# A decoder layer with three attention branches: causal masks moved from TensorE to the softmax bias and into a scan, and the first feed-forward products reordered

## The chip, the cores and the metric

The kernel runs on one core of one Trainium2 chip. Its engines are TensorE (PE in the profile, its weight loads PEld), VectorE (DVE), ScalarE (ACT), GpSimd (POOL) and SyncE (SP, which issues most DMAs). Each engine works through its own queue in order; semaphores order the engines against each other. The metric is the device time of one execution in microseconds (us), the median of several runs.

## The reference

One layer, 1024 tokens of width 1024, all in float32:

```python
proj = x @ w_in            # queries, keys, values of three branches, an index head group, gates
o_a  = sparse attention    # top-256 keys by the index score, softmax with ALiBi, 8 heads
o_b  = forgetting attention # softmax(q k / 8 + c_q - c_k), causal: key <= query, 8 heads
# stick-breaking, 8 heads, strictly causal (key < query):
z = q k / 8
log_one_minus = where(key < query, log_sigmoid(-z), 0)
later = reverse cumulative sum of log_one_minus, without the element itself
a = where(key < query, exp(log_sigmoid(z) + later), 0)
o_c = a v
merged = sum over branches of (o_i w_branch_i) * sigmoid(gates_i)
x  = LN1(alpha * x + merged w_out)
h  = relu(x w_ff1) ** 2
out = LN2(alpha * x + h w_ff2)
```

## The kernel before, in words

Dense products are done in three parts: each float32 operand is split into a high part (a conversion on ACT or POOL) and a low part (a subtraction on DVE or POOL), and hi*hi, hi*lo and lo*hi are added up in PSUM. `split` and `Weights.convert` do this; `wraw` is the weight as loaded, `whi` and `wlo` its parts.

The kernel has these stages: transposing x; the index products and scores; the three attention branches in the order Fox (forgetting), Stick (stick-breaking), Dsa (sparse), with the projections and gates of the input matrix run between their steps as filler; the branch products; the output product with the first layer norm; the first feed-forward product; the second one.

An attention unit (`Unit`) is one head and two query tiles of 128 rows (`u` from 0 to 3, tiles 2u and 2u+1). Its steps: `qk` makes the scores of one row tile against all keys up to its diagonal, in one or two PSUM banks named `l` (two exist); `rows` turns them into weights; `tr` transposes pairs of blocks on PE into banks named `t` and splits them into `ph` and `pl`; `pv` multiplies with the values into a bank `o`.

In `qk` the causal mask is a third product into the same bank: the weights `negeye` (-1e30 on the diagonal, bf16) times a triangle of ones, `tri_excl` (keys after the query) for Fox and for the first two tiles of Dsa, `tri_incl` (the query's own key too) for Stick.

`softmax_rows` (Fox and Dsa) adds the bias and takes the running extreme on DVE, `tensor_tensor_reduce`, which the profile calls CUSTOM_DVE_ANT_0 (out `p`, and `nm` for the extreme). Then the exponential runs on ACT, the reciprocal of the sum on DVE, and the scaling on POOL (`p<-p,sm`). Fox's bias `ct` is one row of 1024 running sums, broadcast to 128 partitions by a DMA, one tile a head; Dsa's `bt` is made on POOL. In Stick, ACT makes two sigmoids `u` and `be`, DVE runs a scan from the last key to the first (`u<-u,zero`), and POOL multiplies.

What stands where in a queue is decided in two steps. A planner (`Plan`) keeps a clock for each engine with written-out costs; `drive` picks the attention step that is ready on that clock, or a step of filler. A search for the top-256 threshold of each query row (`select`: 33 rounds of six counts `jk`, then six passes that write the bias into `score`) is put in the background of DVE wherever the planner sees a gap; what is left when Dsa needs a row is emitted at once. The framework then orders each engine's instructions by its own list scheduling.

The first feed-forward product is done with seven block products per group of 256 columns instead of eight, from sums and differences of blocks of x (`x1` to `x7`, each as `h` and `l`) and of the weights (`hl`); `PSTEPS` is the order of the products. The blocks of x come from transposes of the normalised rows (`transpose_row`, evicted to `mr`) and their sums (`sums`). For the last row tile this happens inside the loop over `PSTEPS`, at step 2, followed by all splits of blocks 5, 7, 4 and 3.

## Time and profile before

| | |
|---|---|
| runs | 2045.75 us median of 3 (2042.17 to 2050.64) |
| profiled execution | 2043.96 us, of which the span from first to last instruction is 2042.2 us |
| granted TensorE clock, mean of the span | 0.995 of full speed |
| PE busy | 2007.3 us (98%) |
| DVE busy | 1391.3 us (68%) |
| ACT busy | 981.8 us (48%) |
| POOL busy | 479.7 us (23%) |

Busy time is the union of an engine's instructions. Products on PE overlap, so the length of one is more than the time between two starts. A time in square brackets behind a row is the engine's idle time ahead of it, with the instruction that ended it. The granted clock is given as a share of full speed; the two levels are 1.2 and 2.4 GHz.

### The profile page before, as it was taken

The numbers are of one execution on the slowest core, as the hardware profiler recorded it, in microseconds if no ns is written. First come the engines' busy times: TensorE is split into PE (matmuls) and PEld (weight loads), VectorE is DVE, ScalarE is ACT, GpSimd is POOL, SyncE is SP. The second block draws the span as 40 slices with busy tenths as digits, with TensorE's granted clock in tenths as the row PEclk, the third lists the DMA queues.
The fourth block names the chain that finished last, engine by engine and source line by source line (L and its number), as shares of the span: only waits on it lengthen the run. The fifth ranks groups of instructions, "written<-read, shape, count | busy, mean of one in ns | idle before, by whom it ended". The sixth has DMA issues, their size and how long they took to land. (4 is left out here: it accounts for less than half of the span.)

```text
span 2042.2 us, 30020 instructions
## 1 busy us (share of the span) xinstructions
PE 2007.3 (98%) x10534; PEld 1693.5 (83%) x10534; DVE 1391.3 (68%) x2501; ACT 981.8 (48%) x1913; POOL 479.7 (23%) x460
## 2 busy tenths in 40 slices
PE   8999999999999999999999999999999999999998
PEld 7788889888888888878988888887877787888886
DVE  3785487777788888764343356767788866875557
ACT  5573454445464464344454443445444445644443
POOL 3312322333353453554354204000000000000003
PEclk9999999999999999999999999999999999999999
DMA  5434534344234334243352586621699845986653
GB/s 158 101 78 99 122 88 122 91 116 108 69 94 120 75 83 116 68 112 91 83 118 74 161 283 204 223 73 46 238 331 347 324 147 196 332 270 191 195 176 124
DMA packets 210327, 308.71 MB, mean 151 GB/s; under 512 B 22248, under 2 KB 116456, under 8 KB 208128
## 3 DMA queue, kind: packets, MB, share of 16 engines
q1 hardware_dynamic: 196032, 281.09, 46.5%
q10 hardware_dynamic: 14144, 25.70, 3.5%
q8 instruction: 83, 1.36, 0.3%
q14 instruction: 68, 0.56, 0.1%
HBM read 182.89 MB, written 79.79 MB: 129 GB/s over the span
## 5 line engine op out<-in xcount | busy, mean ns | idle before, releaser
L138 PE MATMUL d<-xh,whi 128*128 128x512 f32 (+1 forms) x912 | 316.8, 399 | 3.5 <-ACT g__9749 L138 1.2
L138 PE MATMUL d<-xh,wlo 128*128 128x512 f32 (+1 forms) x912 | 312.0, 393 | 0.0
L138 PE MATMUL d<-u 128*128 128x512 f32 x1320 | 303.0, 391 | 2.5 <-ACT u L138 1.8
L138 PE MATMUL d<-xl,whi 128*128 128x512 f32 (+1 forms) x912 | 304.8, 385 | 0.0
L138 PEld LDWEIGHTS d<-u 128*128 128x128 f32 x1320 | 248.4, 188 | 56.9 <-ACT u L138 3.2
L138 POOL TENSOR_TENSOR wlo<-wraw,whi 128x512 fp32r<-128x512 f32 x138 | 196.8, 1429 | 386.9 <-ACT whi L138 345.2
L138 DVE TENSOR_TENSOR u<-sr,u 128x512 fp32r<-128x512 f32 x220 | 144.7, 702 | 91.1 <-ACT u L138 90.9
L138 DVE TENSOR_TENSOR pl<-t,ph 128x512 fp32r<-128x512 f32 (+1 forms) x240 | 146.6, 630 | 85.8 <-ACT ph L138 85.5
L138 ACT ACTIVATE u<-sr 128x512 fp32r<-128x512 f32 x220 | 130.1, 627 | 142.0 <-PE d L138 105.4
L138 PEld LDWEIGHTS d<-xl,whi 128*128 128x128 f32 x912 | 172.4, 189 | 30.9
L138 POOL TENSOR_TENSOR z<-z,res 128x512 f32<-128x512 f32 x14 | 19.7, 1429 | 748.0 <-ACT z L138 733.1
L138 PEld LDWEIGHTS d<-xh,whi 128*128 128x128 f32 x912 | 167.6, 190 | 29.6 <-DVE st L138 2.2
L138 DVE TENSOR_SCALAR_CACHE_REDUCE jk<-sc,fb 128x384 uint8<-128x384 f32 (+2 forms) x198 | 186.2, 940 | 3.4
L138 PEld LDWEIGHTS d<-xh,wlo 128*128 128x128 f32 x912 | 164.2, 190 | 25.6
L138 ACT ACTIVATE ph<-t 128x512 fp32r<-128x512 f32 (+1 forms) x240 | 127.7, 558 | 94.3 <-PE t L138 88.7
L138 ACT ACTIVATE p<-p,nm 128x896 f32<-128x896 f32 (+7 forms) x128 | 99.3, 776 | 148.7 <-DVE nm L138 132.5
L138 ACT ACTIVATE whi<-wraw 128x512 fp32r<-128x512 f32 x136 | 86.3, 634 | 160.3 <-PE d L138 114.0
L138 POOL TENSOR_SCALAR p<-p,sm 128x896 f32<-128x896 f32 (+7 forms) x128 | 98.6, 772 | 147.1 <-DVE sm L138 143.4
L138 DVE TENSOR_TENSOR_SCAN u<-u,zero 128x128 f32<-128x128 f32 (+3 forms) x64 | 110.5, 1737 | 24.0 <-ACT u L138 23.2
L138 PE MATMUL o<-ph,v 128*128 128x256 f32 x480 | 121.5, 278 | 0.0
L138 PE MATMUL o<-pl,v 128*128 128x256 f32 x480 | 118.2, 284 | 1.9 <-DVE pl L138 1.5
L138 ACT ACTIVATE mr<-mr 128x512 f32<-128x512 f32 x110 | 69.3, 630 | 85.7 <-DVE mr L138 83.6
(274 smaller groups left out, 4394.5 us busy)
## 6 DMA issues: line engine op xcount, KB each, us to landing
wraw<-in_w_in_dram SPq DMA_DIRECT2D x136, 256.0 KB, 3.0
sr<-h_scratch SPq DMA_DIRECT2D x112, 256.0 KB, 3.3
w1raw<-in_w_ff_dram SPq DMA_DIRECT2D x16, 1024.0 KB, 6.8
h_scratch<-mr SPq DMA_DIRECT2D x64, 256.0 KB, 3.6
w2raw<-in_w_ff_dram SPq DMA_DIRECT2D x16, 1024.0 KB, 7.7
t_scratch<-w2raw SPq DMA_DIRECT2D x16, 1024.0 KB, 8.1
sr<-t_scratch SPq DMA_DIRECT2D x64, 256.0 KB, 4.0
oraw<-o_scratch SPq DMA_DIRECT2D x24, 512.0 KB, 4.9
```

The lines of the kernel that those rows point to most:

```text
L138: r = f(*args, **kw)
```

## The change

- `qk` has no mask product any more; `negeye` and both triangles are gone.
- Fox: the mask is written into the bias. A head's units run from u = 3 down to 0 and a unit's tiles from the higher to the lower (`down`). At a head's first row POOL writes -1e30 over the part of the last 128-column block of `ct` that lies after the query (`diagonal`); after the reduction of row i, and ahead of its exponential, it does the same to the block before, for row i-1. The blocks behind need no repair, since lower rows don't read them. `prepare` loads the next head's `ct` one head ahead.
- Dsa: for the first two tiles POOL writes the mask into `bt`; the others had no mask product.
- Stick: the scan runs over the keys 1 to w-1, with maximum in place of addition and a byte tile `newest` in place of zeros. `newest` holds a one at each query's newest key, so that the running product begins there, and zeros elsewhere. The last column of `be` is set to zero by a memset on DVE.
- First feed-forward: the last row tile is transposed at step 1, PE's products 1 to 5 are pinned in order behind its transposes, and the splits of blocks 5, 7, 4 and 3 are spread over steps 3, 4, 6 and 7.
- Small things: `zero` and `bf` share a tile, as do `fb`, `mb`, `cnt` and `need` (`sel`).

The diff, cut to its core:

```diff
-    negeye = cp.tile([P, P], BF16, name="negeye")
-    V.tensor_scalar(negeye, ident, -BIG, None, op0=ALU.mult)
-    tri_incl = cp.tile([P, P], BF16, name="tri_incl")
-    tri_excl = cp.tile([P, P], BF16, name="tri_excl")
-    for t_, cmp in ((tri_excl, ALU.is_gt), (tri_incl, ALU.is_ge)):
-        V.memset(t_, 1.0)
-        G.affine_select(t_, t_, pattern=[[1, P]], compare_op=cmp, fill=0.0, base=0,
-                        channel_multiplier=-1)
+    newest = cp.tile([P, S], U8, name="newest")
+    def diagonal(t_, cmp, fill):
+        G.affine_select(t_, t_, pattern=[[-1, P]], compare_op=cmp, fill=fill, base=0, channel_multiplier=1)
...
+    one = plan.tile(ap, [P, S], F32, tag="T", bufs=2, name="one")
+    V.memset(one, 0.0)
+    G.affine_select(one[:, S - P - 1:S - 1], one[:, S - P - 1:S - 1], pattern=[[-1, P]],
+                    compare_op=ALU.not_equal, fill=1.0, base=0, channel_multiplier=1)
+    V.tensor_copy(newest, one)
...
@@ -519,11 +523,8 @@
         cut = min(w, 384 if w == 640 else 512)
         for c, tag in zip((slice(0, cut), slice(cut, w))[:1 + (cut < w)], tags):
             dst = bank(tag, 2)[:, :c.stop - c.start]
-            last = mask is not None and c.stop == w
             for n, (q, k) in enumerate((first, second)):
-                T.matmul(dst, q[:, qs], k[:, c], start=n == 0, stop=n == 1 and not last)
-            if last:
-                T.matmul(dst[:, i * P - c.start:], negeye, mask, start=False, stop=True)
+                T.matmul(dst, q[:, qs], k[:, c], start=n == 0, stop=n == 1)
             out.append((c, dst))
         return out
...
-    def softmax_rows(lg, i, bias):
+    def softmax_rows(lg, i, bias, then=None):
         w = (i + 1) * P
         p = row_tile(i, "p")
         sm = plan.tile(ap, [P, 1], F32, tag="sm", bufs=4, name="sm")
@@ -566,24 +567,36 @@
             nm = plan.tile(ap, [P, 1], F32, tag="nm", bufs=4, name="nm")
             V.tensor_tensor_reduce(p[:, c], l_, bias[:, c], -SCALE, m, ALU.add, ALU.min, nm)
             m = nm
+        if then:
+            then()
         A.activation(p[:, :w], p[:, :w], AF.Exp, bias=nm, scale=-1.0, accum_out=sm)
         V.reciprocal(sm, sm)
         G.tensor_scalar(p[:, :w], p[:, :w], sm, 0.0, op0=ALU.mult, op1=ALU.add)
         return p
     class Fox:
-        branch, mask = 1, lambda self, i: tri_excl
+        branch, down = 1, True
+        def __init__(self):
+            self.ct = []
         def prepare(self, h):
-            ct = plan.tile(ap, [P, S], F32, tag="T", bufs=2, name="ct")
-            Q.dma_start(ct, c_dram[h:h + 1, :].broadcast_to([P, S]))
-            return ct
+            for n in range(len(self.ct), min(NH, h + 2)):
+                self.ct.append(plan.tile(ap, [P, S], F32, tag="T", bufs=2, name="ct"))
+                Q.dma_start(self.ct[n], c_dram[n:n + 1, :].broadcast_to([P, S]))
+            diagonal(self.ct[h][:, S - P:], ALU.is_ge, -BIG)
+            return self.ct[h]
         def rows(self, lg, i, h, ct):
-            return softmax_rows(lg, i, ct[:, :(i + 1) * P])
+            def mask():
+                if i > 0:
+                    diagonal(ct[:, (i - 1) * P:i * P], ALU.is_ge, -BIG)
+            return softmax_rows(lg, i, ct[:, :(i + 1) * P], mask)
     class Stick:
-        branch, mask = 2, lambda self, i: tri_incl
+        branch, down = 2, False
         prepare = pre = None
         def rows(self, lg, i, h, _):
@@ -593,13 +606,16 @@
             for c, l_ in lg:
                 A.activation(u[:, c], l_, AF.Sigmoid, scale=-SCALE)
                 A.activation(be[:, c], l_, AF.Sigmoid, scale=SCALE)
-            V.tensor_tensor_scan(u[:, :w][:, ::-1], u[:, :w][:, ::-1], zeros(P, w), 1.0,
-                                 ALU.mult, ALU.add)
+            V.tensor_tensor_scan(u[:, 1:w][:, ::-1], u[:, 1:w][:, ::-1], newest[:, S - w:S - 1][:, ::-1], 0.0,
+                                 ALU.mult, ALU.max)
+            V.memset(be[:, w - 1:w], 0.0)
             G.tensor_tensor(be[:, :w - 1], be[:, :w - 1], u[:, 1:w], ALU.mult)
             return be
     class Dsa:
-        branch, mask = 0, lambda self, i: None if i in TI else tri_excl
+        branch, down = 0, False
         prepare = pre = None
         def rows(self, lg, i, h, _):
...
                        allow_small_or_imprecise_dtypes=True)
             G.tensor_scalar(bt[:, :w], d, -slope / SCALE, 0.0, op0=ALU.mult, op1=ALU.add)
+            if i not in TI:
+                diagonal(bt[:, i * P:w], ALU.is_ge, -BIG)
             return softmax_rows(lg, i, bt[:, :w])
     class Unit:
...
+        def tile(self):
+            n = len(self.p)
+            return 2 * self.u + (1 - n if self.kind.down else n)
         def qk_ready(self):
             pr, r = self.pair, self.h % 2
-            return max(qk_slot(2 * self.u + len(self.p)), plan.slot(ap, f"P{2 * self.u + len(self.p)}", 1),
+            return max(qk_slot(self.tile()), plan.slot(ap, f"P{self.tile()}", 1),
                        plan.ready(pr["q"][r], pr["qs", r], pr["k"][r]))
         def qk(self):
             k = self.kind
             n, pr, r = len(self.p), self.pair, self.h % 2
-            if n == 0 and self.u == 0 and k.prepare:
+            if n == 0 and self.u == 3 * k.down and k.prepare:
                 k.pre = k.prepare(self.h)
-            i = 2 * self.u + n
-            lg = qk((pr["q"][r], pr["k"][r]), (pr["qs", r], pr["k"][r]), i, k.mask(i))
-            self.p.append(k.rows(lg, i, self.h, k.pre))
+            i = self.tile()
+            lg = qk((pr["q"][r], pr["k"][r]), (pr["qs", r], pr["k"][r]), i)
+            self.p.insert(0 if k.down else n, k.rows(lg, i, self.h, k.pre))
         def tr_ready(self):
             return max(plan.slot(ps, "t", 2), plan.slot(ap, "ph", 2), plan.ready(*self.p))
...
@@ -812,12 +833,13 @@
-    def order(first):
-        return [(r, u) for v in range(2) for r in range(2) for u in (2 * v, 2 * v + 1)] if first else \
-            [(r, u) for r in range(2) for u in range(4)]
+    def order(k, p):
+        if k is kinds[2] and p == 0:
+            return [(r, u) for v in range(2) for r in range(2) for u in (2 * v, 2 * v + 1)]
+        return [(r, u) for r in range(2) for u in (range(3, -1, -1) if k.down else range(4))]
     units = [Unit(k, 4 * n + p, pairs[4 * n + p], 2 * p + r, u) for n, k in enumerate(kinds)
-             for p in range(NPAIR) for r, u in order(n == 2 and p == 0)]
+             for p in range(NPAIR) for r, u in order(k, p)]
     qks = [(m, n) for m in range(len(units)) for n in range(2)]
     trs = [(m, jp) for m, un in enumerate(units) for jp in range(un.u + 1)]
     st = {"qk": 0, "tr": 0, "pv": 0, "swap": 0}
...
@@ -1297,17 +1322,24 @@
     AHEAD = 3
     W2_AT = [16 + 6 * n for n in range(NPR)]
+    LATER = {3: (b11, 5), 4: (b12, 7), 6: (b21, 4), 7: (b22, 3)}
     prepare1(2)
     for m in range(len(PSTEPS)):
-        if m == 2:
-            transpose_row(NT - 1, (A, V))
+        if m == 1:
+            behind = transpose_row(NT - 1, (A, V))
             sums(3)
-            for src, j in ((b11, 5), (b12, 7), (b21, 4), (b22, 3)):
-                for c in range(4):
-                    ts_ = slice(c * P, (c + 1) * P)
-                    split(*(v[:, :, ts_] for v in x1v[j]), src[:, :, ts_])
+        if m in LATER:
+            src, j = LATER[m]
+            for c in range(4):
+                ts_ = slice(c * P, (c + 1) * P)
+                split(*(v[:, :, ts_] for v in x1v[j]), src[:, :, ts_])
         prepare1(m + AHEAD)
-        product1(m)
+        if 1 <= m <= 5:
+            with tc.issue_after(behind.ins):
+                behind = product1(m)
+        else:
+            product1(m)
         evacuate1(*PSTEPS[m])
         if m == W2_AT[0] - 2:
             rctx.close()
```

Where the instructions stand, before and after. First POOL in Fox, around the change from one head's rows to the next's (`p<-p,sm` is the scaling of one row tile, its width the row's; `wlo<-wraw,whi` the low part of a filler weight). Before:

```order
L138 TENSOR_SCALAR p<-p,sm 128x1024
L138 TENSOR_TENSOR wlo<-wraw,whi 128x512
L138 TENSOR_SCALAR p<-p,sm 128x128
L138 TENSOR_SCALAR p<-p,sm 128x256
L138 TENSOR_SCALAR p<-p,sm 128x384
L138 TENSOR_SCALAR p<-p,sm 128x512
L138 TENSOR_TENSOR wlo<-wraw,whi 128x512
```

After, from row tile 3 of the first head to row tile 6 of the second:

```order
L138 TENSOR_SCALAR p<-p,sm 128x512
L138 TENSOR_SCALAR p<-p,sm 128x384
L138 AFFINE_SELECT ct<-ct 128x128
L138 TENSOR_TENSOR wlo<-wraw,whi 128x512
L138 TENSOR_SCALAR p<-p,sm 128x256
L138 TENSOR_SCALAR p<-p,sm 128x128
L138 AFFINE_SELECT ct<-ct 128x128 x2
L138 TENSOR_SCALAR p<-p,sm 128x1024
L138 TENSOR_TENSOR wlo<-wraw,whi 128x512
L138 AFFINE_SELECT ct<-ct 128x128
L138 TENSOR_SCALAR p<-p,sm 128x896
```

The rows run downwards now, and between the scalings stand the selects that write the mask for the next row; the first of the two selects that stand together at a head's begin belongs to another head's bias.

Second PE at the first feed-forward products, at the first product with block 6 of x (`x1`, `x2`, `x6` name the block; each product is a run of twelve). Before:

```order
L138 MATMUL d<-x1l,hl 128x512
L138 MATMUL d<-x1h,hl 128x512
L138 MATMUL d<-x6h,hl 128x512
L138 MATMUL d<-x6l,hl 128x512
L138 MATMUL d<-x6h,hl 128x512 x2
L138 MATMUL d<-x6l,hl 128x512
```

After:

```order
L138 MATMUL d<-x2h,hl 128x512 x2
L138 MATMUL d<-x2l,hl 128x512
L138 MATMUL d<-x2h,hl 128x512
L138 MATMUL d<-x6h,hl 128x512
L138 MATMUL d<-x6l,hl 128x512
L138 MATMUL d<-x6h,hl 128x512 x2
L138 MATMUL d<-x6l,hl 128x512
```

Before, block 6 follows the second product of block 1; now the second product of block 2 stands between them.

Third DVE in the same place (`x5l`, `x7l`, `x4l`, `x3l` are the low parts of blocks of x, `hl` those of weights, `s` and `w1raw` sums of weights, `mr<-d,early` an eviction). Before:

```order
L138 TENSOR_TENSOR x6l<-t_15155,x6h 128x4x128
L138 TENSOR_TENSOR x5l<-mr,x5h 128x4x128 x2
L138 TENSOR_TENSOR x7l<-mr,x7h 128x4x128 x4
L138 TENSOR_TENSOR x4l<-mr,x4h 128x4x128 x4
L138 TENSOR_TENSOR x3l<-mr,x3h 128x4x128 x4
L138 TENSOR_TENSOR hl<-w1raw,hl 128x512
L138 TENSOR_TENSOR hl<-s_15098,hl 128x512
L138 TENSOR_TENSOR mr<-d,early 128x512
L138 TENSOR_TENSOR s_15339<-w1raw 128x512
L138 TENSOR_TENSOR w1raw<-w1raw 128x4x128 x3
```

After:

```order
L138 TENSOR_TENSOR x6l<-t_15310,x6h 128x4x128
L138 TENSOR_TENSOR x5l<-mr,x5h 128x4x128 x4
L138 TENSOR_TENSOR hl<-s_15253,hl 128x512
L138 TENSOR_TENSOR x7l<-mr,x7h 128x4x128 x4
L138 TENSOR_TENSOR s_15478<-w1raw 128x512
L138 TENSOR_TENSOR mr<-d,early 128x512
L138 TENSOR_TENSOR w1raw<-w1raw 128x4x128
L138 TENSOR_TENSOR x4l<-mr,x4h 128x4x128
L138 TENSOR_TENSOR w1raw<-w1raw 128x4x128
L138 TENSOR_TENSOR x4l<-mr,x4h 128x4x128 x2
L138 TENSOR_TENSOR hl<-w1raw,hl 128x512 x2
L138 TENSOR_TENSOR x4l<-mr,x4h 128x4x128
```

Before, all sixteen low parts of blocks 5, 7, 4 and 3 stand ahead of the next weights; now those of block 4 stand among the weight sums, and those of block 3 further behind.

## Rows read from the trace of the kernel before

**Rows 1.** The page: busy time of PE, and its share in 40 slices (tenths).

```profile
PE 2007.3 (98%) x10534; PEld 1693.5 (83%) x10534; DVE 1391.3 (68%) x2501; ACT 981.8 (48%) x1913; POOL 479.7 (23%) x460
...
PE   8999999999999999999999999999999999999998
```

**Rows 2.** Busy time by stretch: start:end, then its length and the engines' shares.

```profile
core 0: us, PE busy (x) PEld busy (x) DVE busy (x) ACT busy (x) POOL busy (x), PEclk, DMA share, GB/s
200.00:525.00 325.00, 324.51 (x1984) 282.21 (x1983) 223.01 (x605) 147.66 (x309) 96.86 (x102) 1.00 0.42 104
525.00:790.00 265.00, 262.50 (x1610) 223.75 (x1609) 222.91 (x313) 156.28 (x348) 127.86 (x98) 1.00 0.36 88
790.00:900.00 110.00, 104.28 (x595) 90.58 (x594) 89.15 (x170) 36.39 (x77) 46.33 (x49) 0.97 0.43 103
900.00:1110.00 210.00, 210.00 (x1260) 185.61 (x1259) 87.70 (x249) 99.98 (x207) 97.00 (x124) 1.00 0.38 93
...
1398.00:1424.00 26.00, 22.44 (x91) 16.71 (x90) 24.87 (x45) 17.51 (x35) 0.00 (x0) 0.93 0.11 42
```

**Rows 3.** Instructions that read `negeye`: shortest, median and longest in ns.

```profile
L138 PE MATMUL l<-tri_excl,negeye x80: 229/230/233, 221.8 to 1109.8; 128*128 128x128 bf16 x80
L138 PE MATMUL l<-tri_incl,negeye x64: 229/230/234, 531.9 to 779.1; 128*128 128x128 bf16 x64
```

**Rows 4.** PE in order of time at a mask: start, length in us.

```profile
222.14 0.23 PE L138 MATMUL l<-tri_excl,negeye 128*128 128x128 bf16 x1
222.18 0.48 PE L138 MATMUL d<-xh,whi 128*128 128x512 f32 x1
222.50 0.39 PE L138 MATMUL d<-xl,whi 128*128 128x512 f32 x1
```

**Rows 5.** PE in order of time behind index scores, which have no mask.

```profile
47.12 0.40 PE L138 MATMUL d<-xh,whi 128*128 128x512 f32 x1
47.36 0.39 PE L138 MATMUL d<-xl,whi 128*128 128x512 f32 x1
47.59 0.39 PE L138 MATMUL d<-xh,wlo 128*128 128x512 f32 x1
```

**Rows 6.** Instructions on the tile `score` (`sc`): counts on DVE, selects on POOL.

```profile
L138 DVE TENSOR_SCALAR_CACHE_REDUCE jk<-sc,fb x198: 580/938/1281, 176.5 to 830.6; 128x384 uint8<-128x384 f32 x33, 128x512 uint8<-128x512 f32 x33, 128x640 uint8<-128x640 f32 x33, 128x768 uint8<-128x768 f32 x33
...
L138 POOL TENSOR_SCALAR_AFFINE_SELECT sc<-sc x6: 292/679/1007, 170.7 to 176.4; 128x128 f32<-128x128 f32 x6
```

**Rows 7.** POOL's waits in Fox, 200 to 525: total us, times, longest.

```profile
POOL wlo L138 <- ACT whi L138: 85.7, 22, 25.1
```

**Rows 8.** The tile `ct`, Fox's bias: its eight loads.

```profile
DMA to landing us min/median/max: 3.4/4.5/5.7
```

**Rows 9.** Instructions on the tile `zero`: scans of Stick, a one-column memset.

```profile
L138 DVE TENSOR_TENSOR_SCAN u<-u,zero x64: 414/1749/3848, 533.9 to 780.6; 128x128 f32<-128x128 f32 x8, 128x256 f32<-128x256 f32 x8, 128x384 f32<-128x384 f32 x8, 128x512 f32<-128x512 f32 x8
...
L138 DVE MEMSET zero<- x1: 59/59/59, 0.9 to 0.9; 128x1 f32 x1
```

**Rows 10.** PE's waits from 790 to 900, the begin of Dsa.

```profile
PE l L138 <- DVE nm L138: 4.4, 3, 2.5
```

**Rows 11.** PE and DVE in order of time at the first feed-forward products.

```profile
1398.86 0.39 PE L138 MATMUL d<-x1h,hl 128*128 128x512 f32 x1
...
1402.07 0.85 PE L138 MATMUL d<-ident,row 128*128 128x128 f32 x5 [0.33 <-DVE row L138]
...
1410.20 0.50 PE L138 MATMUL d<-x6h,hl 128*128 128x512 f32 x1 [1.43 <-ACT x6h L138]
1411.35 0.74 PE L138 MATMUL d<-x6l,hl 128*128 128x512 f32 x1 [0.64 <-DVE x6l L138]
...
1414.82 2.49 DVE L138 TENSOR_TENSOR x4l<-mr,x4h 128x512 fp32r<-128x512 f32 x4
...
1417.23 2.49 DVE L138 TENSOR_TENSOR x3l<-mr,x3h 128x512 fp32r<-128x512 f32 x4
...
1425.61 0.40 PE L138 MATMUL d<-x6h,hl 128*128 128x512 f32 x1
```

More of the change, by code (lines that the diff above doesn't have):

```diff
@@ L189, in trunk @@
     make_identity(nc, ident)
-    zero = cp.tile([P, 1], F32, name="zero")
+    both = cp.tile([P, 2], F32, name="both")
+    zero, bf = both[:, 0:1], both[:8, 1:2]
     V.memset(zero, 0.0)
     A.activation(zero, zero, AF.Copy)
-    negeye = cp.tile([P, P], BF16, name="negeye")
-    V.tensor_scalar(negeye, ident, -BIG, None, op0=ALU.mult)
-    tri_incl = cp.tile([P, P], BF16, name="tri_incl")
-    tri_excl = cp.tile([P, P], BF16, name="tri_excl")
-    for t_, cmp in ((tri_excl, ALU.is_gt), (tri_incl, ALU.is_ge)):
-        V.memset(t_, 1.0)
-        G.affine_select(t_, t_, pattern=[[1, P]], compare_op=cmp, fill=0.0, base=0,
-                        channel_multiplier=-1)
+    newest = cp.tile([P, S], U8, name="newest")
+    def diagonal(t_, cmp, fill):
+        G.affine_select(t_, t_, pattern=[[-1, P]], compare_op=cmp, fill=fill, base=0, channel_multiplier=1)
     def split(hi, lo, src, eng=V, first=A):
@@ L478, in first_block @@
         V.tensor_copy(wi, tb[:, :len(TI) * IDXH].rearrange("p (i h) -> p i h", i=len(TI)))
-    bf = cp.tile([8, 1], F32, name="bf")
     spread = "h (c s) -> (h c) s"
@@ L511, in cumulate, with qk @@
         Q.dma_start(c_dram, t2)
-    def qk(first, second, i, mask, tags=("l", "l")):
+    def qk(first, second, i, tags=("l", "l")):
         w = (i + 1) * P
@@ L545, in emit @@
             rl = row_tile(i, "rl")
-            for c, lg in qk((dst["q"][r], kis), (dst["q"][r], kil), i, None, tags):
+            for c, lg in qk((dst["q"][r], kis), (dst["q"][r], kil), i, tags):
                 A.activation(rl[:, c], lg, AF.Relu)
@@ L656, in pv_ready @@
         def pv_ready(self, jp):
-            f = plan.slot(ps, "o", 1) if self.u % 2 == 0 and jp == 0 else 0.0
+            f = plan.slot(ps, "o", 1) if self.u % 2 == self.kind.down and jp == 0 else 0.0
             return max(f, plan.ready(*self.pt[jp]))
@@ L661, in pv @@
             u, h, k = self.u, self.h, self.kind
-            if u % 2 == 0 and jp == 0:
+            if u % 2 == k.down and jp == 0:
                 k.ob = bank("o", 1)
@@ L672, in pv @@
                 T.matmul(o[:, q0:], st, pl[:, s_], start=False, stop=jp == u and jj == 1)
-            if u % 2 == 1 and jp == u:
+            if u % 2 != k.down and jp == u:
                 t_ = plan.tile(dp, [P, 512], F32, tag="o", bufs=NO, name="o")
@@ L684, in trunk @@
     NI = len(TI)
-    fb = cp.tile([P, NI], I32, name="fb")
-    mb = cp.tile([P, NI], I32, name="mb")
-    cnt = cp.tile([P, NI], F32, name="cnt")
-    need = cp.tile([P, NI], F32, name="need")
+    sel = cp.tile([P, 4, NI], F32, name="sel")
+    fb, mb = (sel[:, n, :].bitcast(I32) for n in range(2))
+    cnt, need = sel[:, 2, :], sel[:, 3, :]
     selected = [TI[0]]
@@ L1056, in transpose_row @@
             for k in range(4):
-                T.transpose(tb[:, k * P:(k + 1) * P], rows[i][:, (4 * g + k) * P:(4 * g + k + 1) * P], ident)
+                t_ = T.transpose(tb[:, k * P:(k + 1) * P], rows[i][:, (4 * g + k) * P:(4 * g + k + 1) * P],
+                                 ident)
             for k in range(4):
@@ L1064, in transpose_row @@
                     V.tensor_scalar(dst, src, g1[:, n:n + 1], b1[:, n:n + 1], op0=ALU.mult, op1=ALU.add)
+        return t_
     def first_tokens(i):
@@ L1235, in product1 @@
             for j, (w_, x_) in enumerate(((wh, xh_), (wh, xl_), (wl, xh_))):
-                T.matmul(b, w_[:, k, :], x_[:, k, :], start=i in FIRST and k == j == 0,
-                         stop=k == 3 and j == 2, skip_group_check=True)
+                r = T.matmul(b, w_[:, k, :], x_[:, k, :], start=i in FIRST and k == j == 0,
+                             stop=k == 3 and j == 2, skip_group_check=True)
+        return r
     w2raw = {}
```

## The prediction, made before the kernel after was run

> **What bounds the kernel now.** I read the page's engine lines first: TensorE (PE) is busy 2007 of 2042 us and no slice of its row falls below 8 [rows 1]. So the span is PE's own work plus some 35 us in which it stands, and an edit counts in two ways only: it takes work off PE, or it makes PE stand. Next the windows by stage [rows 2]: PE is idle 0.5 us in the stage of the forgetting branch (200 to 525 us, Fox), 2.5 us in that of the stick-breaking branch (525 to 790), 5.7 us where the sparse branch (DSA) begins (790 to 900, granted clock 0.97), and 3.6 us in the first 26 us of the feed-forward part (1398 to 1424, clock 0.93). VectorE (DVE) is the next engine: 223 of 325 us in Fox, 223 of 265 in Stick, 24.9 of 26 at the start of the feed-forward. GpSimd (POOL) has work for 97 us of Fox's 325.
>
> **The masks that leave PE.** 144 bf16 products, 80 of one triangle and 64 of the other, each shown as 0.23 us long [rows 3]. But products overlap, so I take the price from starts. With a mask, the start of the mask lies 0.36 us ahead of the start of the second product behind it (222.14, 222.18, 222.50) [rows 4]; without one, the same dense product takes 0.24 us from its start to the next one's (47.12, 47.36) [rows 5]. The mask takes 0.36 - 0.24 = 0.12 us, of which 0.04 is its own slot and 0.08 is added to the product behind it. 144 x 0.12 = 17.3 us. The ends: 144 x 0.04 = 5.8 if that 0.08 were paid without a mask too (the unmasked rows say it isn't), 144 x 0.23 = 33 if each cost its whole shown length (the starts say it doesn't). All of it lies on PE, and nothing covers it.
>
> The Trainium skill, page "TensorE: Matmul & The Clock Gate", section "Back-to-back issue gap", speaks against so large a saving: 128 columns take 134 cycles at the full clock, and a steady stream of weight load and product some 81 ns. By its cycles (56 ns) the 144 masks would be worth an estimated 8 us, by its stream 12 us, and the sum below would end near 2037 or 2033. The trace doesn't agree here: 0.12 us between the starts.
>
> **Fox: selects and turned rows.** A head's rows now run from the last query tile to the first, and between two of them POOL writes -1e30 over one 128x128 block of the bias. That is 64 selects, and the reduction of the next row on DVE waits for its own. One select of that size took 0.29 to 1.01 us [rows 6]; 64 x 0.29 = 19 to 64 x 1.0 = 64 us, on an engine with 228 us free in Fox. On the path it can lie like this: reduction of row i, select, reduction of row i-1. The select starts when row i's reduction ends, and so does row i-1's score product, since it needs the same PSUM bank; both last well under a microsecond, so they run side by side. Behind a waiting reduction DVE's queue holds the splits and reciprocals that PE's next products need. DVE idles 102 us over 64 rows, 1.6 us a row, which is the cover. Two things can use it up: a weight split of POOL ahead of the select (POOL waited 22 times for ScalarE's half of it, 85.7 us in all [rows 7]), and the next heads' bias, which six selects at the head of POOL's queue now wait for (3.4 to 5.7 us from issue to landing [rows 8]). At the low end the cost is 0; at the high end, 64 rows that each pass on a quarter of a microsecond, 16 us. I take 1.5, near the row for PE's idle time in this stage, 0.5 us. The turned order itself changes no instruction count; I take nothing for it, between -0.5 (all idle time of the stage) and the ends just given.
>
> **Stick.** The scan keeps its length less one element and its two inputs; one is now a byte tile and the second operation a maximum. The scans before run 0.41 to 3.85 us at 128 to 1024 columns [rows 9]. No row has this form. If nothing changes it costs 0; if each of the 64 were a tenth slower on a 1.75 us median, 11 us of DVE. The added memsets of one column are 64 x 0.06 = 3.8 us of DVE [rows 9]. DVE has 42 us free there, so I take 1 us, with ends -1 and +8. The background search for thresholds, which fills DVE's gaps, is displaced by whatever is added.
>
> **Start of DSA.** PE waits 4.4 us here for DVE's reductions [rows 10], because the rest of the search is forced ahead of them. After the change four counts fewer stand ahead of the first DSA reduction in DVE's order; at 0.94 us each [rows 6] that is 3.8 us more to force, part of it hidden. I take +1, with ends -4 (the waits fall otherwise) and +4. The 16 new selects on DSA's first two tiles lie on POOL, 46 of 110 us busy, or later, where PE is idle 0.0 us of 210 [rows 2]: nothing.
>
> **First feed-forward products.** From the first x1 product (1398.86) to the first x6 product of the second column group (1425.61) lie 26.75 us [rows 11] for 84 products and 8 transposes. At 0.23 us a product [rows 5] and some 1.2 us for the transposes (five in 0.85) that is 20.5 us of work, so 6.2 us are lost: waits of 0.33, 1.43, 0.64 us and others behind them, and a lower clock after them. DVE sets these. Its queue ran the splits x4l and x3l, 2.49 us each, ahead of the weights of x5. Now all eight transposes come at once, the second group's x2 product goes ahead of x6, which moves x6's and x5's need back by 2.7 us, and x4l and x3l stand behind. But the next x6 needs its weights from DVE: x7l, which ended at 1414.8, comes 1.3 us later (two weight splits now precede it), and nine instructions of 0.62 stand from there to the weights, 5.6 us: 1421.7. So I expect x6 there instead of at 1425.6, 4 us earlier, with a PE wait of some 2 us left. Ends: 0 (fewer DVE instructions stand ahead of that point, so it is not later) and 6.2.
>
> The new constants at the start lie beside the load of x.
>
> **Sum.** -17.3 - 4 + 1.5 + 1 + 1 = -17.8 us. The profiled execution took 2043.96 us, so 2026.2; the median of the runs lies 1.8 above it, so 2028.
>
> **Rivals.**
> *Selects eat half or more of the gain.* Each Fox row passes 0.15 to 0.3 us to PE, 10 to 19 us: 2036 to 2045. For: DVE's queue is in order and POOL's splits wait often [rows 7]. Against: 1.6 us of DVE idle a row.
> *Masks are cheap.* Only their own 0.04 us goes: -5.8 - 4 + 3.5 = -6.3, so 2039. For it speaks the slot that a mask shows, against it rows 5.
> *Slower: POOL's weight splits hold the selects.* Place: Fox, 22 waits of POOL for ScalarE of 3.9 us each (85.7 / 22). A select behind one holds a reduction, and beyond 1.6 us DVE holds PE: 2.3 us a time. All 22: 51 us, 2043.96 - 21.3 + 51 + 1.8 = 2075. It decides the sign from 21.3 + 10 = 31 us, 14 of the 22 on. Against: in POOL's order after the change most selects follow a normalising pass, few a weight split.
> *More: the start of DSA runs free.* The stall of 5.7 us and the clock (3% of 110 us) vanish: 9 to 10 us more, near 2017.
> That the masks stay is no rival: the program after has none of the 144.
>
> **Chances.** Forecast (gain of 11 to 24 us) 0.62; selects eat the gain 0.17; masks cheap 0.05; slower 0.06; more 0.10. About 0.5%, 10 us, is what a measurement can tell from no change. Faster 0.62 + 0.10 = 0.72; same 0.17 + 0.05 = 0.22; slower 0.06. The range for 8 in 10 reaches from 2016 (DSA running free) to 2044 (most of the second rival); the likeliest case alone spans 2020 to 2035.
>
> **What would show it.** Right: no bf16 product on PE, PE's busy time lower by more than 10 us, its idle time in Fox under 3 us, the second x6 some 4 us sooner after the first x1. Wrong in the second or fourth case: PE waiting in Fox for DVE's `pl` or `nm`, and DVE waiting for POOL's `ct`. Wrong in the third: the dense product behind an unmasked score product takes 0.32 us instead of 0.24. Wrong on Stick: scans above the lengths of before.

## The result: 10 to 12 us faster, and where they lie

The changed kernel takes 2032.6 us (median of five runs, 2031.2 to 2036.9); the kernel before took 2045.0 beside it (five runs). By the medians it is 12 us faster. The estimated ratio is 0.9949, with an interval of 0.9933 to 0.9965: about 10 us, between 7 and 14. That is clear of zero, and about as much as the 10 us that the prediction called the least that can be told. The forecast was 2028, a gain of 18 us. The time is near, the gain is 60 to 70% of the forecast's, and two of its terms were far off, in opposite directions.

The profiled execution is the slowest of its five runs: 2036.9 us, span 2035.1 against 2042.2. The page of the changed kernel, to be read beside [rows 1]:

```profile
PE 1990.4 (98%) x10390; PEld 1693.7 (83%) x10390; DVE 1378.1 (68%) x2564; ACT 979.5 (48%) x1913; POOL 506.5 (25%) x539
...
PE   8999999999999999989999999999999999999998
...
PEclk9999999999999999989999999999999999999999
```

PE is busy 17 us less, but the span is only 7 us shorter. The windows, with the columns of [rows 2], say where PE stands instead:

```profile
200.00:525.00 325.00, 323.90 (x1971) 286.90 (x1970) 222.63 (x614) 150.94 (x313) 114.44 (x165) 1.00 0.42 104
525.00:790.00 265.00, 256.05 (x1499) 221.71 (x1499) 215.97 (x366) 152.67 (x342) 129.94 (x97) 0.99 0.37 90
790.00:900.00 110.00, 101.95 (x575) 88.73 (x574) 86.82 (x163) 34.02 (x73) 46.02 (x51) 0.92 0.41 101
900.00:1110.00 210.00, 209.21 (x1245) 184.42 (x1244) 86.67 (x251) 100.21 (x209) 101.14 (x134) 1.00 0.37 93
1400.00:1426.00 26.00, 25.02 (x112) 19.76 (x111) 24.99 (x45) 20.03 (x39) 0.00 (x0) 1.00 0.11 41
```

PE's idle time in Fox is 1.1 us (0.5 before) and in Stick 9.0 (2.5). In the DSA start it is 8.1 (5.7), at a granted clock of 0.92 (0.97). PE's longest waits between 200 and 1180 us, as total us, times and longest:

```profile
PE l L138 <- DVE nm L138: 6.2, 3, 3.3
PE o L138 <- DVE pl L138: 5.4, 6, 1.5
PE l L138 <- ACT be L138: 2.7, 4, 1.0
```

The wait of a score bank for ScalarE's `be` is new. All waits of this stretch sum to 18.4 us, those of before to 8.0. The clock adds to them: between 535 and 1150 us, 26 dense products of 512 columns start 0.42 to 0.44 us after the one ahead of them without a wait between, where most start 0.23 us after it. Before there were 10 of them. That is the lower of the two clock levels, and some 3 us more of it.

The instructions on the tile `ct` (shortest, median and longest in ns) give the selects, and below them who waited for one (us, times):

```profile
L138 POOL TENSOR_SCALAR_AFFINE_SELECT ct<-ct x64: 287/293/305, 88.1 to 474.8; 128x128 f32<-128x128 f32 x64
...
  DVE p L138: 0.7, 1
```

The instructions on `newest` give the scans:

```profile
L138 DVE TENSOR_TENSOR_SCAN u<-u,newest x64: 417/1576/3065, 527.8 to 785.4; 128x127 f32<-128x127 f32 x8, 128x255 f32<-128x255 f32 x8, 128x383 f32<-128x383 f32 x8, 128x511 f32<-128x511 f32 x8
```

Those on `be` give the memsets:

```profile
L138 DVE MEMSET be<- x64: 59/59/59, 531.1 to 788.2; 128x1 f32 x64
```

A select takes 0.29 us, and the reductions waited for one only once, 0.7 us. (Six selects waited for their bias's load, 19.2 us of GpSimd in all, and still the reductions waited only that once.) The scans are no longer than [rows 9]. At the first feed-forward products PE shows this, to be read beside [rows 11]:

```profile
1400.60 0.39 PE L138 MATMUL d<-x1h,hl 128*128 128x512 f32 x1
...
1411.16 0.50 PE L138 MATMUL d<-x2h,hl 128*128 128x512 f32 x1 [0.69 <-ACT early L138]
...
1414.01 0.39 PE L138 MATMUL d<-x6h,hl 128*128 128x512 f32 x1
...
1422.17 0.39 PE L138 MATMUL d<-x6h,hl 128*128 128x512 f32 x1
```

The second group's x6 follows the first x1 by 21.6 us (26.75 before).

The table gives each profiled execution in stages (us): Fox, from the first score product to the first transposition of a Stick row; Stick and DSA, to the last transposition; the stretch to the first x1 product; from there to the second group's x6; from there to the first product of the second feed-forward matrix (FF2); and to the end. Stick and DSA stand together, because the planner moves dense products across their border: the last column counts those that start within Stick, from its first transposition to its last. A ratio is to executions of the kernel before that were taken with the run (their medians lie between 2044.5 and 2046.1). The runs fox_alone and stick_back are the same program up to the x1 products and differ by 2.7 us in Stick and DSA: that is the scatter of one execution, and a smaller difference in this column says nothing.

| run | median | ratio, interval | Fox | Stick+DSA | to x1 | x1-x6 | x6-FF2 | to end | dense |
|---|---|---|---|---|---|---|---|---|---|
| before | 2045.0 | | 320.6 | 614.4 | 243.2 | 26.8 | 303.6 | 313.0 | 708 |
| changed | 2032.6 | 0.9949, 0.9933-0.9965 | 314.1 | 622.2 | 243.8 | 21.6 | 300.8 | 312.2 | 764 |
| masks_out | 2045.1 | 1.0003, 0.9990-1.0016 | 318.1 | 618.1 | 244.1 | 26.7 | 305.2 | 310.5 | 752 |
| masks_out_billed | 2035.5 | 0.9948, 0.9932-0.9965 | 313.0 | 612.2 | 244.5 | 27.4 | 305.1 | 312.5 | 708 |
| masks_unbilled | 2053.5 | 1.0040, 1.0026-1.0054 | 324.9 | 625.2 | 244.9 | 26.7 | 301.5 | 310.4 | 752 |
| stick_back | 2028.7 | 0.9920, 0.9902-0.9938 | 314.6 | 614.8 | 244.9 | 21.6 | 299.6 | 310.2 | 708 |
| after_billed | 2028.1 | 0.9920, 0.9906-0.9934 | 314.1 | 613.4 | 244.7 | 21.6 | 299.5 | 312.5 | 708 |
| memset_early | 2042.2 | 0.9987, 0.9975-0.9998 | 314.1 | 625.7 | 245.3 | 21.6 | 297.6 | 312.7 | 776 |
| fox_alone | 2038.9 | 0.9969, 0.9957-0.9980 | 314.5 | 612.1 | 245.8 | 27.4 | 304.3 | 310.4 | 708 |
| ff1_back | 2041.4 | 0.9982, 0.9971-0.9994 | 314.1 | 621.2 | 243.9 | 27.4 | 300.6 | 311.0 | 764 |
| ff1_only | 2034.5 | 0.9950, 0.9934-0.9966 | 320.6 | 613.7 | 245.0 | 21.8 | 297.8 | 312.0 | 708 |
| counts_short | 2019.4 | 0.9875, 0.9856-0.9893 | 312.4 | 608.9 | 244.3 | 21.6 | 297.9 | 311.3 | 708 |
| bg_fox | 2026.8 | 0.9916, 0.9895-0.9938 | 314.5 | 612.5 | 245.4 | 21.6 | 299.2 | 311.9 | 720 |
| bg_both | 2027.2 | 0.9918, 0.9896-0.9940 | 314.5 | 612.0 | 244.2 | 21.6 | 301.3 | 311.3 | 708 |

Stick and DSA lost 80 masks and became 7.8 us longer. That is the puzzle that the runs were for.

### The profile page after: what moved, and what is told of

Its sections match the earlier page's. It is cut to its first block, busy times and chain, and to the rows that moved or that the text cites. A ratio compares the mean times of both kernels' runs of the same rounds, so it can differ in the third digit from the quotient of the medians.

```text
span 2035.1 us, 29911 instructions
## 1 busy us (share of the span) xinstructions
PE 1990.4 (98%) x10390; PEld 1693.7 (83%) x10390; DVE 1378.1 (68%) x2564; ACT 979.5 (48%) x1913; POOL 506.5 (25%) x539
## 5 line engine op out<-in xcount | busy, mean ns | idle before, releaser
L138 POOL TENSOR_TENSOR wlo<-wraw,whi 128x512 fp32r<-128x512 f32 x138 | 201.6, 1464 | 358.6 <-ACT whi L138 317.7
L138 DVE TENSOR_SCALAR_CACHE_REDUCE jk<-sc,sel 128x384 uint8<-128x384 f32 (+2 forms) x198 | 186.3, 941 | 3.2
L138 ACT ACTIVATE p<-p,nm 128x1024 f32<-128x1024 f32 (+7 forms) x128 | 99.4, 776 | 152.1 <-DVE nm L138 148.4
L138 DVE TENSOR_TENSOR_SCAN u<-u,newest 128x127 f32<-128x127 f32 (+3 forms) x64 | 105.5, 1656 | 22.7 <-ACT u L138 22.0
L138 POOL TENSOR_SCALAR p<-p,sm 128x1024 f32<-128x1024 f32 (+7 forms) x128 | 99.7, 781 | 69.9 <-DVE sm L138 63.5
```

What stands on the lines that cost most here:

```text
L138: r = f(*args, **kw)
```

## Experiments

**Masks left out, and Stick put back.** The first theory was that the memset behind the scan holds GpSimd's multiplication and so Stick.

```diff
# masks_out: in the kernel before, for Fox, Stick and DSA
-branch, mask = 1, lambda self, i: tri_excl
+branch, mask = 1, lambda self, i: None
# stick_back: in the changed kernel, for Stick
+T.matmul(dst[:, i * P - c.start:], negeye, mask, start=False, stop=True)
...
-V.tensor_tensor_scan(u[:, 1:w][:, ::-1], ..., newest[...], 0.0, ALU.mult, ALU.max)
-V.memset(be[:, w - 1:w], 0.0)
+V.tensor_tensor_scan(u[:, :w][:, ::-1], ..., zeros(P, w), 1.0, ALU.mult, ALU.add)
```

Masks_out:

> The kernel before, with the 144 mask products left out and nothing in their place (the three branches then attend to later keys inside the diagonal block; this part of the computation is changed). It prices the masks alone, without selects, memsets or the byte scan. Theory M (a mask costs 0.12 us of TensorE wherever it stands): 17 us less than before, about 2028; the Stick stage (from its first transposition to its last score product) falls from 256.8 to about 249 us. Rival C (Stick is limited by its chain ScalarE, scan, GpSimd multiplication, so that its 64 masks only filled waits): the Stick stage stays at 255 to 257, TensorE's idle time there rises from 2.5 to about 9 us, the whole gains about 10 us, 2035. Rival S (only the mask's own slot of 0.04 us goes): 2039.

Stick_back:

> The changed kernel with the stick-breaking branch alone as it was: mask products on TensorE, scan over zeros from 1.0, no memset. Theory W (the memset between scan and GpSimd's multiplication makes Stick stall): the Stick stage returns from 269.2 to 257 us and TensorE's idle time there from 9 to 2.5 us, the start of DSA to 5.7 us; the whole falls by 8 to 14 us against the changed kernel, to 2019 to 2025. Rival T (the byte scan takes more of the port that it shares with GpSimd): the same here; only the run with the early memset tells it from W. Rival N (the extra stalls belong to the one profiled execution or to the planner's order in general): Stick stays near 265, the whole at 2030 to 2040.

Masks_out gained nothing at all (ratio 1.0003), less than any theory allowed, without select, memset or byte scan. Its PE waits between 200 and 1180 us, first four groups:

```profile
PE l L138 <- DVE nm L138: 7.5, 7, 2.5
PE d L138 <- DVE st L138: 5.5, 5, 1.3
PE l L138 <- ACT be L138: 3.5, 2, 1.9
PE o L138 <- DVE pl L138: 3.1, 9, 0.4
```

All groups sum to 22.1 us, 14 more than before. Stick_back lies between W and N: some 4 us faster than the changed kernel by the medians, with 64 masks more on PE; its waits sum to 10.4 us. So taking Stick's masks off costs time in the changed kernel; and masks_out, with neither memset nor byte scan, shows that these are not needed for masks to be worth nothing.

**The memset moved.** In the changed kernel it goes ahead of the sigmoids:

```diff
+V.memset(be[:, w - 1:w], 0.0)
 for c, l_ in lg:
-    A.activation(be[:, c], l_, AF.Sigmoid, scale=SCALE)
+    e = min(c.stop, w - 1)
+    A.activation(be[:, c.start:e], l_[:, :e - c.start], AF.Sigmoid, scale=SCALE)
-V.memset(be[:, w - 1:w], 0.0)
```

> The changed kernel with the memset of the last column set ahead of ScalarE's sigmoids (which then leave that column out), so that GpSimd's multiplication waits for the scan alone, as before. The byte scan stays. Theory W (the memset behind the scan is the wait): the Stick stage falls from 269.2 to 249 to 258 us, TensorE's idle time there from 9 to under 4, the whole to 2018 to 2025. Rival T (the byte scan itself disturbs GpSimd): no change, Stick 267 to 270, 2030 to 2035. Rival C (chain-limited): Stick 256 to 262 with waits for ScalarE's sigmoid left.

It was 10 us slower by the medians, outside every expectation. The number of dense products in Stick changed again (776), and PE's waits between 200 and 1180 us sum to 23.6 us. So the run had changed two things: where the memset waits, and the whole order that the planner makes.

**The order and the masks apart.** The planner adds 0.056 us for a mask to TensorE's ledger (the clock that `Plan` keeps for an engine) and picks the next instruction by these ledgers. Take the mask away and 2146 of TensorE's 10,392 other instructions change places. So each was varied alone:

```diff
# masks_out_billed: the kernel before, charge without the mask
-T.matmul(dst[:, i * P - c.start:], negeye, mask, start=False, stop=True)
+plan.account("PE", 0.056, [dst], [])
# masks_unbilled: the kernel before, mask without the charge
+nc.tensor.matmul(dst[:, i * P - c.start:], negeye, mask, start=False, stop=True)
```

Masks_out_billed:

> The kernel before with the 144 mask products left out (later keys of the diagonal block are then attended to: that part of the computation is changed), but with the planner still charging TensorE 0.056 us for each, so that the order of the instructions stays that of the kernel before (6 of its 10,392 other TensorE instructions stand elsewhere; in the run without masks and without the charge, 2146 did). Theory O (the masks are worth their 0.12 us, and what ate it is the other order that the planner makes when the charge is gone): 17 us less than before, 2027 to 2031. Theory C (chain-limited: the same order only waits where the masks stood): 2038 to 2046, TensorE's waits between 200 and 900 us at 18 to 22 us instead of 8.

Masks_unbilled:

> The kernel before with all its 144 masks, whose 0.056 us the planner doesn't charge, so that the order is that of the run without masks (40 of 10,392 TensorE instructions differ). Nothing of the computation is changed. Theory O: the other order costs 10 to 17 us by itself, 2056 to 2063. Theory C: the masks fill the waits that the run without masks showed, 2043 to 2050.

| medians | order of before | order without the charge |
|---|---|---|
| with masks | 2044.5 | 2053.5 |
| without | 2035.5 | 2045.1 (beside 2046.1 for before) |

Each run lies between its two theories, for both are half right. By the medians the order costs 9 to 10 us with or without masks, and the masks are worth 8 to 9 us in either order, half their price. By the ratios, which allow for the different executions of before, both are 8 to 11 us. In masks_out the two cancel. With the order of before and no masks, PE shows at the place of [rows 4]:

```profile
221.26 0.22 PE L138 MATMUL l<-ka,qs 128*128 128x128 f32 x1
...
221.49 0.28 PE L138 MATMUL l<-ka,qs 128*128 128x256 f32 x1
221.61 0.40 PE L138 MATMUL d<-xh,whi 128*128 128x512 f32 x1
221.84 0.39 PE L138 MATMUL d<-xl,whi 128*128 128x512 f32 x1
```

The score product is followed by the second dense product after 0.35 us (221.84 - 221.49). In the kernel before the same score product stands ahead of [rows 4]:

```profile
222.02 0.28 PE L138 MATMUL l<-ka,qs 128*128 128x256 f32 x1
```

There it was 222.50 - 222.02 = 0.48: a mask costs 0.13 us here. Taken like this at every place where both traces have the same neighbours, 63 masks of Fox give back 7.3 us, 64 of Stick 6.6 and 16 of DSA 1.5. Fox keeps its gain: 320.6 to 313.0. Stick and DSA keep 2.2 of their 8.1 us, which is within the scatter. Of PE's waits between 200 and 1180 us these two grew (`st` are parts of a projection); before:

```profile
PE o L138 <- DVE pl L138: 1.5, 4, 0.6
...
PE d L138 <- DVE st L138: 0.9, 2, 0.6
```

With the masks out and charged:

```profile
PE o L138 <- DVE pl L138: 3.6, 7, 0.9
...
PE d L138 <- DVE st L138: 1.3, 2, 0.7
```

Product by product, Stick loses 3.9 us at places without a mask, nearly all of it at products on `pl`, 0.1 to 1.1 us at a time.

**The changed kernel with the ledger as it was.**

```diff
+if billed and c.stop == w:                      # billed: Stick's rows
+    plan.account("PE", 0.056, [dst], [])
...
-V.memset(be[:, w - 1:w], 0.0)
+nc.vector.memset(be[:, w - 1:w], 0.0)           # not entered in the ledger
```

> The changed kernel with two entries of the planner's ledger altered and no instruction added or removed: the stick-breaking rows are still charged 0.056 us of TensorE for a mask, and the memset is charged nothing. TensorE, ScalarE then run in the very order of the run with the stick-breaking masks put back (0 of 10,392 instructions elsewhere). Theory O: that run's 2028.7 less 64 masks of 0.12 us, 2020 to 2023, the Stick stage at 249 to 252 us. Theory C or the memset as a wait: 2028 to 2033, Stick 256 to 262, with waits for pl and be in it.

It beats the changed kernel: 2028.1, ratio 0.9920 against 0.9949. The intervals, from different sets of runs, overlap in the fourth digit (0.9934 and 0.9933), but the six executions (2027.2 to 2030.2) all lie below the five of the changed kernel (2031.2 to 2036.9). It equals stick_back, though, which has the same TensorE order and 64 masks more, and lies where theory C had it. Of theory O the order is right and the price in Stick wrong. Stick_back's window of 525 to 790 us:

```profile
525.00:790.00 265.00, 262.67 (x1601) 223.75 (x1600) 223.69 (x311) 156.91 (x349) 128.59 (x100) 1.00 0.38 92
```

After_billed's:

```profile
525.00:790.00 265.00, 258.29 (x1541) 223.74 (x1540) 225.41 (x376) 156.68 (x349) 128.79 (x100) 1.00 0.38 93
```

PE is busy 4.4 us less and idle 4.4 us more. PE's wait for `pl` between 200 and 1180 us in stick_back:

```profile
PE o L138 <- DVE pl L138: 2.1, 5, 0.6
```

The same in after_billed:

```profile
PE o L138 <- DVE pl L138: 5.8, 10, 1.1
```

Set side by side product by product, the two traces show eight places in Stick where a product on `pl` takes back 0.3 to 1.1 us of what the missing masks had given. At the two longest the order is not the same after all. In one of them GpSimd's weight split stands one place earlier in its queue, ahead of a multiplication of Stick. In stick_back the scan there took:

```profile
605.96 0.69 DVE L138 TENSOR_TENSOR_SCAN u<-u,both 128x256 f32<-128x256 f32 x1
```

In after_billed it runs beside the split, takes 0.83 us longer, and the split `pl` behind it is late:

```profile
605.88 1.30 POOL L138 TENSOR_TENSOR wlo<-wraw,whi 128x512 fp32r<-128x512 f32 x1
...
606.21 1.52 DVE L138 TENSOR_TENSOR_SCAN u<-u,newest 128x255 f32<-128x255 f32 x1
...
608.30 0.55 DVE L138 TENSOR_TENSOR pl<-t,ph 128x384 fp32r<-128x384 f32 x1
...
608.90 0.38 PE L138 MATMUL o<-pl,v 128*128 128x256 f32 x1 [0.94 <-DVE pl L138]
```

In the other a scan of VectorE stands one place earlier, beside the same kind of split (1.78 us instead of 0.90), and PE waits 1.06 us. These 2 us are the framework's other order again; masks_out_billed has the first of them too, its largest loss in Stick. The other six places, 2.5 us together, have the same order on all engines: there PE comes earlier, and `pl` less so.

The 64 memsets and the byte scan are in one of the two traces and not in the other. Outside the places of the masks Stick loses 5.8 us here, and it lost 3.9 us in masks_out_billed, which has neither: at most some 2 us can be theirs, less than the scatter.

**What `pl` waits for: VectorE's load or the chain.** In after_billed each background count is cut to 16 columns, and charged as before:

```diff
...
-V.tensor_scalar(jk[:, :(i + 1) * P], score[i], ...)
+nc.vector.tensor_scalar(jk[:, :16], score[i][:, :16], ...)
+plan.account("DVE", 0.14 + (i + 1) * P / 960, [jk, cnt], [score[i], fb])
...
```

A constant of the search's first comparison is altered as well; no instruction is added or left out by it.

> The run with the mask still charged (after_billed), with each of the 198 background counts shortened to 16 columns while the planner still charges it in full, so that the order of TensorE stays (19 of 10,392 elsewhere). The thresholds of the sparse branch are then other ones: that part of the computation is changed. It tells what the waits in Stick, and those at the start of DSA, stand on. Theory D (VectorE's load: counts in its queue make the splits pl late, and the masks' time went into these waits): VectorE's busy time between 525 and 790 us falls from 225 to about 165 us, TensorE's idle time there from 6.7 to under 2, the Stick stage from 255.9 to 249 to 251 us, and the start of DSA (7.4 us idle) to under 2: the whole 2010 to 2016. Theory L (latency of the chain sigmoid, scan, multiplication, transposition, split, whatever VectorE carries beside it): Stick stays within 2 us, the start of DSA alone gains, 2018 to 2023.

The counts' median fell from 938 to 228 ns. The window of Stick:

```profile
525.00:790.00 265.00, 260.93 (x1554) 225.79 (x1554) 186.96 (x386) 156.75 (x350) 132.76 (x101) 1.00 0.39 96
```

Two of PE's waits (200 to 1180 us):

```profile
PE l L138 <- DVE nm L138: 3.7, 3, 2.6
...
PE o L138 <- DVE pl L138: 1.6, 3, 0.5
```

The wait for `pl` fell to 1.6 us, and Stick and DSA together by 4.5 us. So VectorE's load explains most of that wait, and the counts are the load. But VectorE still carried 187 us instead of the 165 expected, and PE was still idle 4.1 us in Stick and 5.6 at the DSA start (790 to 900; 7.4 in after_billed). The time is that of theory L, the waits for `pl` went as D has it: D holds in part, and the rest of the chain was not taken apart. By the medians the whole gained 8.7 us; what Stick and DSA don't show of it lies in Fox (1.7), where counts run as well, and in the feed-forward part (2.8).

**The parts alone.** Fox_alone undoes Stick and the feed-forward order, ff1_back undoes the latter, and ff1_only applies it to the kernel before (`if m == 1` for `if m == 2`, the splits by `LATER`, `issue_after(behind.ins)`).

Fox_alone:

> Of the change, the bias masks of Fox and of DSA's first two tiles alone (80 masks leave TensorE, rows turned, selects on GpSimd); stick-breaking branch and feed-forward products as before. By the prices 80 x 0.12 = 9.6 us less than before, 1 to 2 us of it lost in Fox: 2036 to 2038. If the feed-forward part gives 8 us in this company as it did beside the changed Stick, the run with the stick-breaking masks put back (2028.7) points to 2037 as well. Theory S (selects eat the gain): 2042 to 2046.

Ff1_back:

> The changed kernel with the first feed-forward products in their former order. Forecast's term: 4 us; the trace of the changed kernel shows 5.2 us from the first x1 product to the second x6 product and 2.8 us more up to the second feed-forward matrix. Theory F (all of it is real): the whole is 5 to 8 us slower than the changed kernel, 2037.5 to 2040.5, nearly all from that stretch. Rival G (the later 2.8 us are chance, or given back): 4 to 5 us slower, 2036.5 to 2037.5. Rival Z (given back wholly): 2033. Stages ahead of the feed-forward part: the same within 2 us by all theories.

Ff1_only:

> The kernel before with the first feed-forward products reordered and nothing else. The forecast's term: 4 us less, 2040.5. The runs with and without it beside the other parts point to 7 to 10 us by the medians (2041.4 against 2032.6, 2038.9 against 2028.7), of which 5.2 to 5.8 us lie between the first x1 and the second x6 product. Theory F (all real, the rest lies in the later feed-forward products): 2035 to 2038. Theory G (the rest is scatter between runs): 2039 to 2040.

Fox_alone gained 6 us, less than the 8 expected: Fox itself took 6.1 us less, and whether DSA's 16 masks kept anything lies within the scatter. Ff1_back was slower than expected (2041.4) and ff1_only faster (2034.5, 10 us): the reorder is worth 7 to 10 us. In ff1_only 4.9 us lie between x1 and x6, and 5.8 between there and the second matrix. PE's waits in this second part in the kernel before (1425 to 1729 us):

```profile
PE d L138 <- DVE mr L138: 2.1, 5, 0.6
PE d L138 <- DVE hl L138: 0.7, 1, 0.7
PE d L138 <- ACT hl L138: 0.6, 1, 0.6
```

All of ff1_only's, from its first x1 product (1399.9) to 1720 us:

```profile
PE d L138 <- ACT early L138: 0.7, 1, 0.7
PE d L138 <- DVE row L138: 0.3, 1, 0.3
```

**More of the search in Fox.** BG holds how much of the search, in us of VectorE, the planner allows by the begin of Fox, by its end and by the end of Stick. In after_billed it is (6, 105, 190), in bg_fox (6, 130, 190) and in bg_both (6, 130, 215).

Bg_fox:

> after_billed with the background search allowed 130 instead of 105 us by the end of Fox, where VectorE idles 102 us: 12 counts (124 instead of 112 of 198) leave Stick for Fox, 11 us of VectorE. The planner's order changes with it (852 TensorE instructions elsewhere). Theory D (VectorE's load in Stick is what waits): 2 to 4 us less than after_billed, 2024 to 2026. Theory L: 2027 to 2029. If Fox has no real cover for them (its reductions wait): 2030 to 2033.

Bg_both:

> The same with 215 instead of 190 us allowed by the end of Stick, so that all 198 counts (196 in after_billed) and part of the selecting passes lie ahead of the first DSA rows. If the forced passes make the start of DSA (7.4 us of TensorE idle, granted clock 0.97): 4 to 6 us less than bg_fox. If VectorE's load makes Stick's waits, Stick loses 3 to 6 us again, and the whole stands at 2024 to 2029.

Neither can be told from after_billed (0.9916 and 0.9918 against 0.9920). Bg_fox is no test of theory D, because the edit didn't take the load where it was meant to: 15 more counts start in Fox (120 against 105), but 64 start in Stick as before, and 7 instead of 22 behind it. PE's waits for `pl` stayed too (6.1 us against 5.8). In bg_both the DSA start's waits became one, and not shorter in sum:

```profile
PE l L138 <- DVE nm L138: 6.5, 1, 6.5
```

## Why the prediction was near, step by step

- **Masks leaving PE, -17.3.** The price was nearly right where it is paid: 143 masks give back 15.4 us at their places, 0.11 each instead of 0.12. The step that failed is "All of it lies on PE, and nothing covers it". In Fox it holds (7.6 us kept). In Stick and DSA the 80 masks had for the most part stood where PE would otherwise wait: 2.2 us kept, within the scatter. The idle times that [rows 2] gave for Stick and the DSA start were what was left with the masks in place, no measure of how close the next wait was.
- **Fox, selects and turned rows, +1.5.** Right: Fox took 314.1 us against 313.0 with the masks merely gone, and the reductions waited once for a select.
- **Stick, +1, and the DSA start, +1.** The largest miss. With their masks gone the two were to become 7.6 us shorter and became 7.8 us longer. The scan and the memset, which the step weighed, cost nothing that stands out of the scatter. What it left out is that the planner no longer charges a mask and does charge a memset, and so makes another order: 56 dense products more in Stick, 10 us more of waits between 200 and 1180, and some 3 us at the lower clock. Putting both entries right gives 4.5 us by the medians (6 by the ratios). "Four counts fewer" ahead of DSA was no cause by itself: after_billed has all 196 again and still waits 5.4 us for `nm`.
- **First feed-forward products, -4.** Mechanism right, size wrong: 5.2 us up to x6, and 7 to 10 with what follows. The step ended its sum at x6 and left out PE's waits behind it, which go as well.
- **The sum.** By the ratios fox_alone gives -6.3, ff1_only -10.2, the two together (stick_back) -16.4, and the Stick part takes back 5.9: -10.5. The forecast had -8.1, -4 and -5.7 for these three parts: the feed-forward term's error of 6 hid half of the 12 us by which the Stick part missed. That the total came as near as it did is luck to this extent.
- **Rivals.** None names the cause. "Selects eat half or more of the gain" (2036 to 2045) begins 3 us above the measured time, but the selects are innocent; "Masks are cheap" fails on the price at the mask and is half true at the end.
- **Signs.** All its signs of being right came: no bf16 product, PE 17 us less busy, 1.1 us idle in Fox, the second x6 5.2 us sooner. None of them bears on Stick, where PE's idle time rose from 2.5 to 9.0 us; the one sign there, longer scans, stayed away. Signs of that kind can't tell a right mechanism from this one.

Open: why the order without the charge is worse, and whether it is by more than chance (a changed ledger moves 852 of TensorE's instructions in bg_fox and 2146 in masks_out, and the charge was varied in two kernels only); which of the two entries matters more; and what makes the rest of Stick's waits.

## What to carry to other kernels

Work on the busiest engine is worth its price only where no other chain is close behind: before removing some, ask of each stage how late its next dependency would be without it, and not only how idle the engine is now. Where a program orders the instructions by modelled costs, removing an instruction also removes its cost from the model: compare the two orders, and run the edit with the old charge kept to part the two effects. Test the parts of a change alone: a total near the forecast here hid errors of 6 and 12 us.

## Unexpected in the hardware

The feed-forward products that read `hl` start 233 ns apart in the kernel before and 227 ns in the changed one. Each line is the first product of a run of twelve in PE's order of time, 2.80 us apart in the kernel before:

```profile
1450.71 0.39 PE L138 MATMUL d<-x3h,hl 128*128 128x512 f32 x1
...
1453.51 0.39 PE L138 MATMUL d<-x5h,hl 128*128 128x512 f32 x1
...
1456.31 0.39 PE L138 MATMUL d<-x7h,hl 128*128 128x512 f32 x1
```

In the changed kernel they are 2.72 us apart:

```profile
1447.05 0.39 PE L138 MATMUL d<-x3h,hl 128*128 128x512 f32 x1
...
1449.77 0.39 PE L138 MATMUL d<-x5h,hl 128*128 128x512 f32 x1
...
1452.49 0.39 PE L138 MATMUL d<-x7h,hl 128*128 128x512 f32 x1
```

The granted clock is 1.00 in both. All five programs with the constants of before show 233, all nine with the changed constants 227, over some 1285 products from the second x6 to FF2: 5 to 6 us of PE, which longer waits took back here (x6 to FF2: 297.8 in ff1_only, 297.6 to 301.3 in the seven runs with both). The constants' sizes shift where `hl` lies in SBUF; that this is the cause was not tested.

A scan is longer where a GpSimd instruction was running already when it began. Of the 64 scans of the changed kernel 31 met 0.2 us or more of such an instruction, and all 31 were longer than the shortest of their width, by 0.1 to 1.5 us. The other 33 were within 0.02 us of the shortest: 19 with no GpSimd work beside them, 10 beside which it began later, and 4 that met the last 0.1 us of it at most. So one over 127 elements took 0.42 us alone and 1.91 us with 1.64 us of a multiplication still to run, while over 895 elements one took 2.02 us alone and another the same beside 1.15 us of a weight split that began after it. The kernel before shows the same, but for one scan of 64, with which a split began in the same instant. The two longest waits for `pl` in after_billed come from such scans.
